# gate_a's matvec on TensorE beside the attention: runs of two slabs at half the rate in place of single slabs

## The chip, the cores and the metric

The kernel runs on one core of a Trainium2 chip. A core has five engines that run side by side, each in the order of its own instruction list: TensorE (PE, matmuls; its weight loads are shown apart as PEld), VectorE (DVE), ScalarE (ACT), GpSimd (POOL) and SyncE (SP), which here only issues DMAs. The metric is the device time of one execution in us.

## The reference

One step of one layer for 128 context tokens and 256 latent tokens, all in float32, model width 2048. Six vectors of 2048 per token group, among them gate_a, come out of a matvec of the condition with a 2048 x 12288 matrix:

```python
def _adaln(cond, ada_w, ada_b):
    mod = jax.nn.silu(cond) @ ada_w + ada_b
    return mod.reshape(cond.shape[0], N_MOD, D_MODEL)

def _layer(x, mod, ...):
    shift_a, scale_a, gate_a, shift_f, scale_f, gate_f = [mod[:, i][:, None, :] for i in range(N_MOD)]
    h = _rmsnorm(x, norm_w[0]) * (1 + scale_a) + shift_a
    q, k, v, o, g, u = jnp.split(h @ w_in, ...)
    hm, C, n, m = _mlstm_bidir(q, k, v, gates, C0, n0, m0)        # attention, 8 heads of 128, two directions
    hm = _rmsnorm(hm, mlstm_norm_w) * jax.nn.sigmoid(o)
    mix = jnp.concatenate([hm, _pool_mixer(u, ...)], axis=-1) @ w_out
    x = x + gate_a * _rmsnorm(mix, norm_w[1])
    h = _rmsnorm(x, norm_w[2]) * (1 + scale_f) + shift_f
    y = jnp.square(jax.nn.relu(h @ w1)) @ w2
    return x + gate_f * _rmsnorm(y, norm_w[3]), C, n, m
```

gate_a is needed only where the output projection is done.

## The kernel before

All 384 tokens go through each stage together. Weights come in tiles of 512 KB, 4 x 128 rows by 256 columns (`load_w`): SP loads a tile into one of three buffers (`raw_q`, `raw_k`, `raw_o`, `raw_wo`), ScalarE rounds it to a high part `hi_...`, VectorE subtracts that for a low part `lo_...` (four buffers each), and TensorE makes three matmuls of each product (lines 143 to 145). A tile's 24 matmuls of 384 columns make one step of a projection (`gemm_T`).

The program goes: the first two modulation vectors and the projections u and v; then, for four groups g of two heads, the projections q and k (`qk(g, ...)`), with the attention of the group before laid between their steps; the projection o in four groups; the output projection wo, in which x stays in 16 tiles; then the MLP. What is laid between the steps of a projection comes from generators. A `Feed` has a rate; after each step it adds the rate to what is due and calls the generator once for each whole number. `fa` holds the attention of the head groups, `ada2` the matvecs for scale_f, shift_f and half of gate_a on VectorE, `ada1` the matvec for the other half of gate_a on TensorE. `ada1` is started with the first projection and is finished in the output projection.

`ada_mat` is TensorE's way: a slab is four rows (of 16 per partition) by 256 columns of the matrix, 512 KB. Per slab there is one load on SP (line 228), and four matmuls (line 232) with a stationary operand of 32 columns, each of which stands in the trace as two records (`ada<-ada_raw,cT 128*32`). gate_a's half has 16 slabs. Behind the last of them ScalarE copies the sums, and two small matmuls (line 241) turn them. `ada_vec` is VectorE's way: a slab is 128 x 1024, one load on SP (line 269) a slab ahead, and two operations of VectorE on it (lines 280 and 282, one for each token group).

Both ways take their slabs from one ring of four buffers, tag "ada" (`N_ADA = 4`): a load waits until the slab of four loads before has been used, whichever engine used it. The order of TensorE, VectorE, ScalarE and SP in this part of the program is made by a scheduler when the kernel is built, from the order in which the code is written and from a model of when operands and buffers come free; it is fixed from then on. SP stands in front of a load until its buffer is free, and every later load on SP stands behind it.

Of the kernel before, what the change touches and what calls it, by code (L numbers as in the profile page):

```python
# [7 lines left out]
F32 = mybir.dt.float32  # L8
# [5 lines left out]
P = 128  # L14
# [13 lines left out]
N_W = 4  # L28
N_ADA = 4
# [10 lines left out]
RATE_MAT = 0.35  # L40
# [3 lines left out]
def hymba_kernel(  # L44
# [6 lines left out]
    nc = tc.nc  # L51
# [3 lines left out]
    wp = ctx.enter_context(tc.tile_pool(name="wp", bufs=3))  # L55
    slots = ctx.enter_context(tc.tile_pool(name="slots", bufs=N_SLOT))
    ada_scope = ExitStack()
    adap = ada_scope.enter_context(tc.tile_pool(name="adap", bufs=1, side="right"))
# [6 lines left out]
    def bank(name):  # L65
        return psum.tile([P, 512], F32, tag="ps", name=name)
# [145 lines left out]
    mod = const.tile([P, 6, KT, 2], F32, name="mod")  # L212
    aw = ada_w.rearrange("(p j) n -> p j n", j=16)

    def ada_mat(parts, tags=("ada",), raws=None):


        n, nk = len(parts), parts[0][2]
        w, nj = nk * P, 8 // nk
        ps = bank(f"ada_{parts[0][0]}_{parts[0][1]}")  # L220
        for b, (i, k0, _) in enumerate(parts):
            c0 = i * D + k0 * P
            for j0 in range(0, 16, nj):
                tag = tags[b % len(tags)]
                raw = raws.pop(0) if raws else None
                if raw is None:
                    raw = (wp if tag == "lo" else adap).tile([P, nj, w], F32, tag=tag, name=f"ada_raw_{i}_{k0}_{j0}", bufs=N_W if tag == "lo" else N_ADA)
                    nc.sync.dma_start(raw, aw[:, j0:j0 + nj, c0:c0 + w])
                for a in range(nj):
                    j = j0 + a  # L230
                    g = j % 4
                    nc.tensor.matmul(ps[32 * g:32 * g + 32, 0:w], cT[:, j, 6 - 2 * b:38 - 2 * b], raw[:, a, :],  # L232
                                     start=b == 0 and j < 4, stop=b == n - 1 and j >= 12)
                if b < n - 1 or j0 + nj < 16:
                    yield
        sb = adap.tile([P, 512], F32, tag="adasb", name=f"ada_sb_{parts[0][0]}_{parts[0][1]}", bufs=1)
        with tc.high_priority():
            nc.scalar.activation(sb[:, 0:w], ps[:, 0:w], AF.Copy)
        yield
        for k in range(nk):  # L240
            nc.tensor.matmul(ps[:, 256 + 8 * k:256 + 8 * k + 2 * n], sb[:, k * P:(k + 1) * P], cst[:, C_SEL, 0:2 * n], start=True, stop=True)
        for b, (i, k0, _) in enumerate(parts):
            ada_finish(i, k0, nk, ps[:, 256:256 + 8 * nk].rearrange("p (k r) -> p k r", r=8)[:, :, 2 * b:2 * b + 2])
        yield

    def ada_finish(i, k0, nk, ps):

        v = mod[:, i, k0:k0 + nk, :]
        nc.vector.tensor_tensor(
            v, ps,  # L250
            abias[:, i, k0:k0 + nk].unsqueeze(2).to_broadcast([P, nk, 2]), op=ALU.add)
        if i in (1, 4):
            w = nw[:, i // 2, k0:k0 + nk].unsqueeze(2).to_broadcast([P, nk, 2])
            nc.vector.scalar_tensor_tensor(v, v, 1.0, w, op0=ALU.add, op1=ALU.mult)
        elif i in (2, 5):
            w = nw[:, 1 if i == 2 else 3, k0:k0 + nk].unsqueeze(2).to_broadcast([P, nk, 2])
            nc.vector.tensor_tensor(v, v, w, op=ALU.mult)
# [50 lines left out]
    def first_ada():  # L308
        for k0, nk in ksteps:
            yield from ada_mat([(0, k0, nk), (1, k0, nk)], ("ada", "lo") if k0 == 0 else ("ada",))  # L310
# [66 lines left out]
    def load_chunk(s, ci, after=(), later=None):  # L377
        kind, c0, w = chunks[ci]
        ks = slice(ksteps[s][0], sum(ksteps[s]))
        if kind == "u":  # L380
            n, pieces = w, [(0, wv_in[:, ks, U0 + c0:U0 + c0 + w])]
        else:
            n, pieces = w * P, [(0, wv_in[:, ks, V0 + c0 * P:V0 + (c0 + w) * P])]
            if c0 == 6:
                pieces.append((n, wv_in[:, ks, 4 * M:4 * M + 32]))
                n += 32
        return load_w(pieces, f"{kind}_{c0}_{s}", ksteps[s][1] * n, after, later) + (n,)
# [9 lines left out]
    for s in range(NS):  # L397
        for ci, (kind, c0, w) in enumerate(chunks):
            k0, nk = ksteps[s]
            hi, lo, n = w_first if s == 0 and ci < 2 else load_chunk(s, ci, h_ins if s == 0 else ())  # L400
# [301 lines left out]
    def mid_vec():  # L702
        for i, q in ((4, 0), (4, 1), (3, 0), (3, 1), (2, 0)):
            yield from ada_vec(i, 1024 * q, 1024)

    ada1 = Feed(ada_mat([(2, 8 + 2 * b, 2) for b in range(4)]), RATE_MAT)
    ada2 = Feed(mid_vec(), RATES[0])

    def qk(g, feeds):
# [92 lines left out]
    for cols in ([0, 256], [512], [768], [1024], [1280], [1536], [1792]):  # L802
        if cols[0] in (768, 1024, 1280):
            for m in range(2):
                n = len(early)
# [71 lines left out]
    def gate_f():  # L877
        yield from ada_mat([(5, 0, 2), (5, 2, 2)], raws=early)
        for q in (1, 2, 3):
            yield from ada_vec(5, 512 * q, 512)  # L880
            if q == 1:
                vec["half"] = True
                while vec["half"]:
                    yield
        ps = bank("gfT")
        t = slot("gfT")[0:32, 0:P]
        nc.tensor.transpose(ps[0:32, 0:P], mod[:, 5].rearrange("p k g -> p (k g)"), ident)
        nc.vector.tensor_copy(t, ps[0:32, 0:P])  # L888
        nc.gpsimd.dma_start(gf_dram, t)  # L889
        yield  # L890
# [409 lines left out]
```

## Time and profile before

The median of three runs is 1694.79 us (1694.71 to 1697.43). The page below is of one execution of 1699.63 us, of which 1697.80 us are the span of the core.

| | us |
|---|---|
| profiled execution | 1699.63 |
| its span | 1697.80 |
| median of 3 runs | 1694.79 |

gate_a's 16 slabs on TensorE start at these times of that execution, in us, with the name that the instruction order gives their load (column tile and row):

| slab | us | slab | us |
|---|---|---|---|
| 8_0 | 225.65 | 8_4 | 245.88 |
| 8_8 | 263.41 | 8_12 | 281.50 |
| 10_0 | 298.42 | 10_4 | 315.10 |
| 10_8 | 334.80 | 10_12 | 346.67 |
| 12_0 | 362.81 | 12_4 | 382.06 |
| 12_8 | 397.23 | 12_12 | 416.10 |
| 14_0 | 436.24 | 14_4 | 450.25 |
| 14_8 | 459.44 | 14_12 | 472.81 |

The state updates of the attention that the prediction speaks of (`cu`) start on TensorE at 278.7, 324.9, 372.6 and 421.0 us, one for each head group.

Rows of the profile begin with the time of the start in us, the duration, the engine and the line; `out<-in` names tiles, x8 says that eight equal records follow each other, and a bracket at the end gives the time for which the engine stood idle ahead of it and who ended that. A row "A <- B: 1.9, 2, 1.1" says that A waited for B 1.9 us in all, in two waits, the longest of 1.1.

### The profile page before, as it was taken

How to read it: one execution, taken by the hardware profiler on the slowest of the kernel's cores; microseconds unless marked ns; L12 is line 12 of the kernel's file. 1: busy time of each engine (PE TensorE's matmuls, PEld its weight loads, DVE VectorE, ACT ScalarE, POOL GpSimd, SP SyncE). 2: the span in 40 equal slices, each digit the busy share in tenths (PEclk: the TensorE clock that was granted, in tenths of full speed). 3: DMA queues.
4: the chain of work that ended last, by engine and by line, in shares of the span. 5: the costliest groups of instructions: out<-in, count | busy, mean ns of one | idle time of the engine just before them, and what ended most of it. 6: DMA issues, size and time to landing. Idle time of an engine off the chain costs nothing.

```text
span 1697.8 us, 28001 instructions
## 1 busy us (share of the span) xinstructions
PE 1664.2 (98%) x11021; PEld 1581.1 (93%) x11021; DVE 1341.8 (79%) x2000; ACT 750.9 (44%) x1224; POOL 155.9 (9%) x194
## 2 busy tenths in 40 slices
PE   6999999999999999999999999999999999999997
PEld 3787899999999989988999999999999999999996
DVE  3676759898989969997798588988588588588688
ACT  4422345545433336453444444344444444444443
POOL 0000001221002223540000000000000000000120
PEclk9999999999999999999999999999999999999999
DMA  8899857777788883754455344544343443533653
GB/s 292 290 298 298 285 164 251 243 242 244 240 271 283 264 264 99 213 161 145 153 180 166 108 149 146 184 150 133 115 141 116 143 129 112 158 112 116 187 183 136
DMA packets 262291, 320.95 MB, mean 189 GB/s; under 512 B 14752, under 2 KB 231440, under 8 KB 261776
## 3 DMA queue, kind: packets, MB, share of 16 engines
q1 hardware_dynamic: 254640, 303.61, 56.8%
q0 software_dynamic: 5856, 13.69, 2.8%
q8 instruction: 86, 1.41, 0.3%
q10 hardware_dynamic: 1664, 1.87, 0.3%
q14 instruction: 45, 0.37, 0.1%
HBM read 308.61 MB, written 10.51 MB: 188 GB/s over the span
## 4 chain that ended last, share of the span: by engine, by line
PE 68%; DVE 15%; DMA 8%; issue 6%; ACT 1%; POOL 1%; SPq 0%; DVEq 0%; ACTq 0%; POOLq 0%
PE acc_w L145 9%; PE acc_w L143 9%; PE acc_w L144 9%; DVE ada_acc L282 6%; PE y L1134 4%; PE y L1135 4%; PE y L1133 4%; PE u L411 2%; DMA raw_u<-in_w_in_dram 2%; PE v L411 2%; PE y_yz L1133 2%; PE y_yz L1134 2%; PE y_yz L1135 2%; PE y L975 2%; PE y L977 2%
## 5 line engine op out<-in xcount | busy, mean ns | idle before, releaser
L144 PE MATMUL acc_w<-h2l,hi_w 128*128 128x384 f32 (+1 forms) x1024 | 345.8, 338 | 0.5 <-DVE h2l L927 0.5
L145 PE MATMUL acc_w<-h2h,lo_w 128*128 128x384 f32 (+1 forms) x1024 | 345.9, 338 | 0.0
L143 PE MATMUL acc_w<-h2h,hi_w 128*128 128x384 f32 (+1 forms) x1024 | 343.8, 337 | 1.3 <-ACT h2h L923 1.2
L135 DVE TENSOR_TENSOR lo_w<-raw_w,hi_w 128x1024 fp32r<-128x1024 f32 x152 | 185.4, 1221 | 135.7 <-ACT hi_w L134 135.6
L282 DVE SCALAR_TENSOR_TENSOR ada_acc<-ada_raw,sg,ada_acc 128x1024 f32<-128x1024 f32 (+1 forms) x240 | 259.9, 1113 | 6.7 <-DMA ada_raw<-in_ada_w_dram 6.7
L134 ACT ACTIVATE hi_w<-raw_w 128x1024 fp32r<-128x1024 f32 x152 | 160.8, 1058 | 211.8 <-PE acc_w L144 93.9
L143 PEld LDWEIGHTS acc_w<-h2h,hi_w 128*128 128x128 f32 x1024 | 192.2, 188 | 2.9 <-ACT h2h L923 2.0
L144 PEld LDWEIGHTS acc_w<-h2l,hi_w 128*128 128x128 f32 x1024 | 192.5, 188 | 1.2 <-DVE h2l L927 0.8
L145 PEld LDWEIGHTS acc_w<-h2h,lo_w 128*128 128x128 f32 x1024 | 192.4, 188 | 0.3 <-DVE lo_w L135 0.2
L1119 ACT ACTIVATE hi_t<-w 128x1024 fp32r<-128x1024 f32 x104 | 109.5, 1059 | 119.0 <-DVE w L1155 34.3
L1120 DVE TENSOR_TENSOR lo_t<-w,hi_t 128x1024 fp32r<-128x1024 f32 x104 | 126.4, 1221 | 14.4 <-ACT hi_t L1119 14.2
L1120 DVE TENSOR_TENSOR lo_b<-w,hi_b 128x1024 fp32r<-128x1024 f32 x78 | 95.2, 1221 | 39.5 <-ACT hi_b L1119 39.3
L1119 ACT ACTIVATE hi_b<-w 128x1024 fp32r<-128x1024 f32 x78 | 82.5, 1059 | 96.0 <-PE acc_w L144 62.3
L134 ACT ACTIVATE hi_wo<-raw_wo 128x1024 fp32r<-128x1024 f32 x32 | 34.0, 1063 | 84.7 <-DMA raw_wo<-in_w_out_dram 57.4
L853 ACT ACTIVATE z<-acc_w 128x384 f32<-128x384 f32 x54 | 26.3, 486 | 74.5 <-PE acc_w L145 74.5
L889 POOL DMA_DIRECT2D gf_dram<-gfT x1 | 0.5, 521 | 552.3 <-DVE gfT L888 552.3
L135 DVE TENSOR_TENSOR lo_wo<-raw_wo,hi_wo 128x1024 fp32r<-128x1024 f32 x32 | 40.4, 1268 | 9.6 <-ACT hi_wo L134 9.5
L411 PE MATMUL v<-hi_v,hh 128*128 128x384 f32 (+1 forms) x144 | 47.8, 332 | 0.0
L411 PE MATMUL v<-hi_v,hl 128*128 128x384 f32 (+1 forms) x144 | 46.5, 323 | 0.0
L411 PE MATMUL v<-lo_v,hh 128*128 128x384 f32 (+1 forms) x144 | 46.5, 323 | 0.0
L232 PE MATMUL ada<-ada_raw,cT 128*32 128x256 f32 x656 | 44.8, 392 | 1.6 <-DMA ada_raw<-in_ada_w_dram 1.5
L134 ACT ACTIVATE hi_u<-raw_u 128x1024 fp32r<-128x1024 f32 x16 | 16.8, 1058 | 63.7 <-DMA raw_u<-in_w_in_dram 62.5
(2250 smaller groups left out, 4602.9 us busy)
## 6 DMA issues: line engine op xcount, KB each, us to landing
ada_raw<-in_ada_w_dram SPq DMA_DIRECT2D x170, 512.0 KB, 4.8
raw_w<-in_w_dram SPq DMA_DIRECT2D x152, 512.0 KB, 4.3
w<-in_w_dram SPq DMA_DIRECT2D x104, 512.0 KB, 4.2
raw_wo<-in_w_out_dram SPq DMA_DIRECT2D x32, 512.0 KB, 5.0
raw_u<-in_w_in_dram SPq DMA_DIRECT2D x16, 512.0 KB, 8.6
raw_q<-in_w_in_dram SPq DMA_DIRECT2D x16, 512.0 KB, 4.8
raw_k<-in_w_in_dram SPq DMA_DIRECT2D x16, 512.0 KB, 4.8
raw_o<-in_w_in_dram SPq DMA_DIRECT2D x16, 512.0 KB, 5.2
```

Source lines behind the costliest of these rows:

```text
L134: nc.scalar.activation(hi[:, 0:n], raw[:, 0:n], AF.Copy)
L135: low = lambda: nc.vector.tensor_tensor(lo[:, 0:n], raw[:, 0:n], hi[:, 0:n].bitcast(F32), op=ALU.subtract)
L143: nc.tensor.matmul(ps, lh, rh, start=start, stop=False)
L144: nc.tensor.matmul(ps, lh, rl, start=False, stop=False)
L145: mm3.ins = nc.tensor.matmul(ps, ll, rh, start=False, stop=stop).ins
L282: nc.vector.scalar_tensor_tensor(acc[:, g, :], raw[:, a, :], cj, acc[:, g, :], op0=ALU.mult, op1=ALU.add)
L411: nc.tensor.matmul(acc[i][:, 0:n], h[k0 + k][a][:, i * P:(i + 1) * P], (hi, lo)[b][:, k, :], start=k == 0 and a + b == 0, stop=k == nk - 1 ...
L1119: nc.scalar.activation(hi, raw, AF.Copy)
L1120: nc.vector.tensor_tensor(lo, raw, hi.bitcast(F32), op=ALU.subtract)
L1133: nc.tensor.matmul(acc, xh, wh, start=start and j == 0, stop=False)
L1134: nc.tensor.matmul(acc, xh, wl, start=False, stop=False)
L1135: nc.tensor.matmul(acc, xl, wh, start=False, stop=stop and j == 3)
```

## The change

`ada_mat` gets an argument `run`. With `run=2` a call of the generator makes two loads, then the eight matmuls of both slabs, and then yields; before, a call made one load and four matmuls. The rate of `ada1` is halved, from 0.35 to 0.175 calls per step, so the two together give the same number of slabs per step. Other callers of `ada_mat` keep `run=1`. In the changed kernel the lines behind 212 have moved: line 228 is 230, 232 is 236, and from there on each line is four higher.

```diff
-    def ada_mat(parts, tags=("ada",), raws=None):
+    def ada_mat(parts, tags=("ada",), raws=None, run=1):
...
         for b, (i, k0, _) in enumerate(parts):
             c0 = i * D + k0 * P
+            ahead = []
             for j0 in range(0, 16, nj):
                 tag = tags[b % len(tags)]
-                raw = raws.pop(0) if raws else None
-                if raw is None:
-                    raw = (wp if tag == "lo" else adap).tile([P, nj, w], F32, tag=tag, name=f"ada_raw_{i}_{k0}_{j0}", bufs=N_W if tag == "lo" else N_ADA)
-                    nc.sync.dma_start(raw, aw[:, j0:j0 + nj, c0:c0 + w])
+                for j1 in range(j0, j0 + nj * run, nj) if not ahead else ():
+                    raw = raws.pop(0) if raws else None
+                    if raw is None:
+                        raw = (wp if tag == "lo" else adap).tile([P, nj, w], F32, tag=tag, name=f"ada_raw_{i}_{k0}_{j1}", bufs=N_W if tag == "lo" else N_ADA)
+                        nc.sync.dma_start(raw, aw[:, j1:j1 + nj, c0:c0 + w])
+                    ahead.append(raw)
+                raw = ahead.pop(0)
                 for a in range(nj):
...
-                if b < n - 1 or j0 + nj < 16:
+                if (b < n - 1 or j0 + nj < 16) and (j0 // nj) % run == run - 1:
                     yield
...
-    ada1 = Feed(ada_mat([(2, 8 + 2 * b, 2) for b in range(4)]), RATE_MAT)
+    ada1 = Feed(ada_mat([(2, 8 + 2 * b, 2) for b in range(4)], run=2), RATE_MAT / 2)
```

On TensorE, the third and the fourth slab (8_8 and 8_12) before: the third stands behind the decays of head group 0 (`mb`), the fourth behind its intra-chunk products (`num`), 91 rows later.

```order
L586 MATMUL mb_0_1_1_2677<-mrow_2080,pick_2081 128x384
L232 MATMUL ada_2_8_2315<-ada_raw_2_8_8_2688,cT_109 32x256 x4
L143 MATMUL acc_q_256_0_2622<-hh4_725,hi_q_256_1_2699 128x384
...
L641 MATMUL num_0_0_1_2867<-v0_85,e_0_2654 128x129 x2
L232 MATMUL ada_2_8_2315<-ada_raw_2_8_12_2881,cT_109 32x256 x4
L143 MATMUL acc_k_1280_0_2899<-hh0_266,hi_k_1280_0_2903 128x384
```

On TensorE after, at the same two places:

```order
L590 MATMUL mb_0_1_1_2677<-mrow_2080,pick_2081 128x384
L143 MATMUL acc_q_256_0_2622<-hh4_725,hi_q_256_1_2693 128x384
...
L645 MATMUL num_0_0_1_2861<-v0_85,e_0_2654 128x129 x2
L236 MATMUL ada_2_8_2498<-ada_raw_2_8_8_2875,cT_109 32x256 x4
L236 MATMUL ada_2_8_2498<-ada_raw_2_8_12_2877,cT_109 32x256 x4
L143 MATMUL acc_k_1280_0_2899<-hh0_266,hi_k_1280_0_2903 128x384
```

The third slab has gone from its place and stands directly ahead of the fourth. All pairs are like this, in the place of their second slab, but for 14_0 and 14_4, which stand together between their two places.

On SP, the loads around 360 to 372 us before. `ada_raw_4_1024_n` is VectorE's n-th slab of the second half of scale_f, `ada_raw_2_12_4` TensorE's slab 12_4, whose neighbour 12_0 has been loaded ten rows earlier.

```order
L269 DMA ada_raw_4_1024_9_3930<-in_ada_w_dram 128x1024
L128 DMA raw_k_1792_1_4022<-in_w_in_dram 128x4x256
L269 DMA ada_raw_4_1024_10_3934<-in_ada_w_dram 128x1024
L128 DMA raw_k_1792_2_4098<-in_w_in_dram 128x4x256
L228 DMA ada_raw_2_12_4_4012<-in_ada_w_dram 128x4x256
L269 DMA ada_raw_4_1024_11_4018<-in_ada_w_dram 128x1024
L269 DMA ada_raw_4_1024_12_4090<-in_ada_w_dram 128x1024
L128 DMA raw_k_1792_3_4132<-in_w_in_dram 128x4x256
```

On SP after, the same place:

```order
L273 DMA ada_raw_4_1024_9_3924<-in_ada_w_dram 128x1024
L273 DMA ada_raw_4_1024_10_3928<-in_ada_w_dram 128x1024
L128 DMA raw_k_1792_1_4022<-in_w_in_dram 128x4x256
L230 DMA ada_raw_2_12_0_4006<-in_ada_w_dram 128x4x256
L128 DMA raw_k_1792_2_4098<-in_w_in_dram 128x4x256
L230 DMA ada_raw_2_12_4_4008<-in_ada_w_dram 128x4x256
L273 DMA ada_raw_4_1024_11_4018<-in_ada_w_dram 128x1024
L128 DMA raw_k_1792_3_4132<-in_w_in_dram 128x4x256
L273 DMA ada_raw_4_1024_12_4090<-in_ada_w_dram 128x1024
```

Both slabs of the pair are loaded here, between VectorE's slabs 10 and 11, and the load of slab 12 has gone behind that of raw_k_1792_3.

On VectorE, the operations around 374 to 380 us before. `nout` and `C1` are the state updates of head group 2, `dn` its denominators:

```order
L282 SCALAR_TENSOR_TENSOR ada_acc_4_1024_3569<-ada_raw_4_1024_11_4018,sg_111,ada_acc_4_1024_3569 128x1024 x2
L282 SCALAR_TENSOR_TENSOR ada_acc_4_1024_3569<-ada_raw_4_1024_12_4090,sg_111,ada_acc_4_1024_3569 128x1024
L683 COPY nout_2082<-C1_2_0_0_3878 128x2
L683 COPY nout_2082<-C1_2_0_1_3885 128x2
L631 SCALAR_TENSOR_TENSOR C1_2_1_0_3892<-C0_2_0_3703,glast_2078,cu_2_1_0_3893 128x129 x2
L655 TENSOR_TENSOR dn_2_0_0_3909<-dn_2_0_0_3909,ecol_2076 128x2
```

On VectorE after:

```order
L286 SCALAR_TENSOR_TENSOR ada_acc_4_1024_3563<-ada_raw_4_1024_11_4018,sg_111,ada_acc_4_1024_3563 128x1024 x2
L687 COPY nout_2082<-C1_2_0_0_3872 128x2
L687 COPY nout_2082<-C1_2_0_1_3879 128x2
L635 SCALAR_TENSOR_TENSOR C1_2_1_0_3886<-C0_2_0_3703,glast_2078,cu_2_1_0_3887 128x129 x2
L286 SCALAR_TENSOR_TENSOR ada_acc_4_1024_3563<-ada_raw_4_1024_12_4090,sg_111,ada_acc_4_1024_3563 128x1024
L635 SCALAR_TENSOR_TENSOR C1_2_2_1_3892<-C0_2_1_3706,glast_2078,cu_2_2_1_3893 128x129 x2
```

The first operation on slab 12 has moved behind the two copies and the first state update. Elsewhere on VectorE single operations on slabs change places with their neighbours in the same way, up to the output projection; none is added or taken away. In the output projection the two small matmuls of line 241 stand 24 matmuls later. From there on the orders of all engines are the same in both kernels.

## The prediction

> **What bounds the kernel now.** I read the page's busy times first, then a table of four stretches, then what TensorE waited for in the stretch that the change touches, then its rows in order of time. The columns of the table are the stretch in us, its length, and busy us of PE, PEld, DVE, ACT and POOL, the granted clock, the DMA share and GB/s.
>
> ```profile
> PE 1664.2 (98%) x11021; PEld 1581.1 (93%) x11021; DVE 1341.8 (79%) x2000; ACT 750.9 (44%) x1224; POOL 155.9 (9%) x194
> 220.00:480.00 260.00, 258.96 (x1674) 245.77 (x1674) 220.89 (x366) 130.43 (x325) 41.85 (x38) 1.00 0.72 229
> 480.00:640.00 160.00, 157.41 (x957) 150.42 (x955) 137.92 (x160) 59.49 (x99) 32.82 (x31) 1.00 0.84 272
> 640.00:1697.80 1057.80, 1045.76 (x6972) 1023.26 (x6970) 845.03 (x1180) 482.59 (x672) 76.52 (x110) 1.00 0.48 146
> ```
>
> TensorE sets the end: it stands idle for 1.0 us of the 260 in which the changed work lies (220 to 480 us), and for 2.6 of the 160 behind it. VectorE is not far off, at 220.9 of 260 and 137.9 of 160. The clock is full, so it explains nothing here. The few idle moments of TensorE between 220 and 640 us are these (line waiting, for whom, us in total, times, longest):
>
> ```profile
> PE acc_wo L145 <- DVE lo_wo L135: 1.9, 2, 1.1
> PE inter L648 <- DVE hs L658: 0.7, 2, 0.5
> PE hT L697 <- DVE hs L661: 0.3, 1, 0.3
> ```
>
> They are small, but nearly all of them are waits for VectorE. At these places both engines arrive together, and time saved on TensorE alone becomes a longer wait there. That is what decides this case.
>
> **The price of a slab.** A slab is one load of gate_a's weights, four matmuls in the program, eight records of the form 128*32 in the trace. One slab alone, behind attention work and ahead of the projection, against the same seam without a slab:
>
> ```profile
> 435.70 0.61 PE L648 MATMUL inter<-C,q 128*128 128x129 f32 x4
> 436.24 0.64 PE L232 MATMUL ada<-ada_raw,cT 128*32 128x256 f32 x8
> 436.81 0.44 PE L143 MATMUL acc_o<-hh,hi_o 128*128 128x384 f32 x1
> 437.09 0.34 PE L144 MATMUL acc_o<-hl,hi_o 128*128 128x384 f32 x1
> ...
> 341.91 0.61 PE L648 MATMUL inter<-C,q 128*128 128x129 f32 x4
> 342.28 0.42 PE L143 MATMUL acc_k<-hh,hi_k 128*128 128x384 f32 x1
> 342.54 0.34 PE L144 MATMUL acc_k<-hl,hi_k 128*128 128x384 f32 x1
> ```
>
> From the first inter matmul to the second projection matmul it is 437.09 - 435.70 = 1.39 us with the slab and 342.54 - 341.91 = 0.63 without: a slab alone costs **0.76 us**. Inside a projection, between two matmuls of the same accumulation, it costs the same:
>
> ```profile
> 245.62 0.34 PE L145 MATMUL poolo<-p21h,lo_pw 128*128 128x384 f32 x1
> 245.88 0.64 PE L232 MATMUL ada<-ada_raw,cT 128*32 128x256 f32 x8
> 246.45 0.45 PE L143 MATMUL acc_k<-hh,hi_k 128*128 128x384 f32 x1
> 246.74 0.33 PE L144 MATMUL acc_k<-hl,hi_k 128*128 128x384 f32 x1
> 246.91 0.33 PE L145 MATMUL acc_k<-hh,lo_k 128*128 128x384 f32 x1
> ```
>
> Here 246.74 - 245.62 = 1.12 us, less two ordinary steps of 246.91 - 246.74 = 0.17, is 0.78. What a second slab directly behind the first costs, gate_f's run of four slabs shows:
>
> ```profile
> 627.50 1.93 PE L232 MATMUL ada<-y,cT 128*32 128x256 f32 x32
> ```
>
> Four slabs take 1.93 us, the first 0.64, so each further one takes (1.93 - 0.64) / 3 = **0.43 us**. The rest of a lone slab's 0.76 is paid at its two borders, where the tile's form changes from 128*128 to 128*32 and back.
>
> **The change, part by part.** The slabs, their last one, and the first reader of gate_a:
>
> ```profile
> L232 PE MATMUL ada<-ada_raw,cT x144: 379/379/404, 225.6 to 632.0; 128*32 128x256 f32 x144
> ...
> 472.81 0.64 PE L232 MATMUL ada<-ada_raw,cT 128*32 128x256 f32 x8
> ...
> 630.54 1.00 DVE L919 SCALAR_TENSOR_TENSOR mo<-mo,mod,tr_r 128x128 f32<-128x128 f32 x3 [1.00 <-PE tr_r L208]
> ```
>
> 144 records, less the 16 of gate_f's two slabs behind 631 us, are 16 slabs of eight. Alone they have 16 borders in and out, in pairs 8. TensorE's work falls by 8 x (0.76 - 0.43) = **2.64 us**; its bounds are 8 x 0, if the second slab pays the price of the first, and 8 x 0.76 = 6.1, if it cost nothing. I take 2.64, as the run of four is the same instruction with the same shape. The number of matmuls, DMAs and bytes is unchanged. The last slab stands at the same place; the two small matmuls that turn the result stand one projection step of 24 matmuls later, and the first reader of gate_a, line 919, starts at 630.5 us, so this is hidden by the whole output projection and costs nothing unless it came over 100 us later.
>
> How much of 2.64 reaches the end I get by following the **lead**, how much earlier the same instruction runs. Each first slab that is gone adds 0.76, each second slab that is added takes back 0.43, and wherever VectorE hands over to TensorE, the lead falls to VectorE's own. VectorE's lead in turn comes from TensorE at the state updates, where VectorE waits for ScalarE's copy of what TensorE has just made (325 us) or for the store of that copy (427 us). The rows of these hand-overs, VectorE's largest waits for POOL and for its own loads in 250 to 480 us, and its load from 500 to 540 us:
>
> ```profile
> 381.42 0.71 PE L648 MATMUL inter<-C,q 128*128 128x129 f32 x4 [0.48 <-DVE hs L658]
> 325.93 0.17 DVE L683 COPY nout<-C 128x2 f32<-128x2 f32 x1 [2.55 <-ACT C L628]
> 427.37 0.61 DVE L631 SCALAR_TENSOR_TENSOR C<-C,glast,cu 128x129 f32<-128x129 f32 x2 [1.49 <-DMA out_dram<-C]
> 524.01 0.44 PE L145 MATMUL acc_wo<-mx12h,lo_wo 128*128 128x384 f32 x1 [1.11 <-DVE lo_wo L135]
> ...
> DVE hs L661 <- POOL rsh L200: 7.0, 12, 0.8
> ...
> DVE ada_acc L282 <- DMA ada_raw<-in_ada_w_dram: 3.3, 3, 1.8
> ...
> 500.00:540.00 40.00, 38.09 (x216) 37.30 (x215) 40.00 (x33) 12.09 (x18) 5.85 (x4) 1.00 0.89 293
> ```
>
> - The slabs' times are in the table of the profile section. At 325 us three pairs are done, 3 x 0.33 = 0.99, but the wait at 308 (0.3 us, above) has already cut the lead by 0.33: TensorE and VectorE both have 0.66.
> - At 381 TensorE has 0.66 + 0.76 - 0.43 + 0.76 = 1.75. VectorE's waits from 330 to there are those of 0.6 to 0.8 for POOL, none for TensorE, so it still has 0.66, and the wait of 0.48 grows to 1.6. Lead 0.66.
> - The pair at 382 takes it to 0.23, the slab gone at 397 to 0.99, the pair at 416 to 0.56. VectorE takes this 0.56 over at 427.
> - By 475 TensorE has 0.56 + 2 x 0.33 = 1.2. VectorE works without a gap in the last row, and at 524 TensorE waits for it: the lead that goes on is **0.56 us**, the wait there grows from 1.1 to about 1.8.
>
> Behind 640 us the order of all engines is the same and TensorE sets the pace, so 0.56 reaches the end. Of the 2.64 saved, 2.1 turn into longer waits. If these waits were no barrier, all 2.64 would get through, and with the 0.48 of the wait at 381 gone too, 3.1.
>
> **The ring of four buffers.** Slabs for TensorE share four buffers with the slabs that VectorE multiplies (line 269). Before, one of the four waits for TensorE; after, two do, from their load to the pair's turn, and VectorE's loads have the other two. Take the second half of the head group at 360 to 382 us. SP's issues, VectorE's uses of what lands, and the times to landing (min, median, max) in this stretch:
>
> ```profile
> 359.89 0.33 SPq L269 DMA_DIRECT2D ada_raw<-in_ada_w_dram  x1
> 364.38 0.38 SPq L228 DMA_DIRECT2D ada_raw<-in_ada_w_dram  x1
> 364.81 4.10 SPq L269 DMA_DIRECT2D ada_raw<-in_ada_w_dram  x2
> ...
> 367.27 1.27 DVE L282 SCALAR_TENSOR_TENSOR ada_acc<-ada_raw,sg,ada_acc 128x1024 f32<-128x1024 f32 x1
> 369.60 2.47 DVE L282 SCALAR_TENSOR_TENSOR ada_acc<-ada_raw,sg,ada_acc 128x1024 f32<-128x1024 f32 x2
> 373.73 3.66 DVE L282 SCALAR_TENSOR_TENSOR ada_acc<-ada_raw,sg,ada_acc 128x1024 f32<-128x1024 f32 x3
> ...
> DMA to landing us min/median/max: 3.2/4.6/7.3
> ```
>
> Before, slab 11 is loaded at 364.8, when TensorE lets its buffer go, and slab 12 at 368.6. After, both wait one release of VectorE longer: slab 11 for the end of the use at 367.27 (368.5), slab 12 for the end of 369.60 + 2.47 (372.1). With 4.6 us they land at 373.1 and 376.7. They are used at 373.73 and, as the third operation from there, at about 376.2; in the new order VectorE does two state copies and an update ahead of it, some 0.7 us. So they are just in time. Of the other seven pairs, worked out alike, two have a load that is late by about half a us. I price the ring at **0** with 0 to 1 us against it; weights behind these loads in SP's queue (raw_k, raw_o) wait for the same releases as before. The cover that hides it is VectorE's other work between two slabs.
>
> The sum: 1699.63 (the profiled execution; its span is 1697.80) - 0.56 = 1699.1. That execution is 4.8 above the median of the three runs, 1694.79; carried to it, **1694.2 us**.
>
> **Rivals.**
> - *All of it gets through.* VectorE's order changes too, and if its hand-overs come earlier, TensorE's 2.64 to 3.1 us reach the end: 1691.7 to 1692.2. For it: VectorE is idle for 39 of the 260 us. Against it: the waits above are all on VectorE, and those at 524 and behind lie in a stretch where it has no gap.
> - *The ring starves VectorE* (the slower side). With two buffers a slab costs VectorE 4.6 for the load, 0.4 for the issue and 2.5 for its two operations, 7.5 us for a buffer's round and so 3.75 per slab, and in the rows above it takes two between 369.6 and about 376.2, one in 3.3. From where two loads in a row miss their use, each pair costs a wait like the one for the load at 467 us, 1.84 us in the row below, handed on at 381, 429 or 524. In four of eight pairs that is 7.4 - 2.6 = 4.8 us: about 1699.6.
>
> ```profile
> 467.58 1.29 DVE L282 SCALAR_TENSOR_TENSOR ada_acc<-ada_raw,sg,ada_acc 128x1024 f32<-128x1024 f32 x1 [1.84 <-DMA ada_raw<-in_ada_w_dram]
> SPq L269 <- DVE ada_acc L282: 106.3, 47, 4.0
> SPq L228 <- DVE ada_acc L282: 23.0, 9, 3.5
> ```
>
> The last two rows show SP standing at these loads until VectorE lets a buffer go, with everything behind them standing too. The Trainium skill, "DMA: Bandwidth & Descriptors", section "Anatomy of one DMA — SWDGE (gpsimd) path", states this as a rule: a DMA engine waits for no semaphore, the wait is made on the issuing sequencer ahead of the dispatch. By that rule two waiting loads in a row hold up the projection's weights as well, and the rival's 1699.6 is what would follow; the trace agrees on where the wait is made, and its single slabs cannot show whether the weights come late.
> - *It does nothing on TensorE.* If the second slab costs 0.76 as well, the sum is 0: 1694.8. Against it stands the run of four.
>
> **How the numbers follow.** Forecast, a small gain of 0 to 1.5 us: 0.55. All gets through (1.5 to 3.1 us): 0.20. Nothing on TensorE: 0.05. Ring or another wait on VectorE costs more than it saves: 0.20, of this 0.13 beyond 0.2%. A difference under 0.2% (3.4 us) can't be told from none here; the three runs of before themselves span 2.7 us. Only a second slab near the bound of no cost gets above 3.4 us: faster 0.10, taken out of the second case; same 0.77; slower 0.13. The range goes from 1691.6, all with the wait at 381, up to 1697.4, the highest run of before and half of the starved ring.
>
> **What would show it.** TensorE's groups of line 236 have 16 records and take about 1.07 us, eight of them; a group of 0.64 twice speaks for the last rival. The waits of lines 648 and 145 behind VectorE (0.7 and 1.9 us) grow to about 2.6 in all at 381 and 524 if the lead is cut as I say, and stay or shrink if all gets through. VectorE's wait for its slabs, 3.3 us in three times, stays below 5; at 10 or more the ring starves. I am wrong if line 128's loads come late or if anything behind 640 us changes.

## The result, and the profile after

The changed kernel takes **1700.16 us** (median of 15 runs, 1698.05 to 1706.83), the kernel before 1696.62 us in the same comparison (15 runs, 1694.71 to 1699.10). The ratio is 1.0025, with a 95% interval of 1.0018 to 1.0033: slower by a quarter of a per cent, where I had forecast 1694.2 and a small gain. Two repeats gave 1.0032 (1.0020 to 1.0044) and 1.0018 (1.0008 to 1.0028).

The page's busy times and the three stretches of the changed kernel, in the columns of the prediction's table:

```profile
PE 1662.1 (98%) x11021; PEld 1582.1 (93%) x11021; DVE 1341.0 (79%) x2000; ACT 752.0 (44%) x1224; POOL 156.4 (9%) x194
220.00:480.00 260.00, 256.04 (x1673) 246.20 (x1672) 221.27 (x368) 130.49 (x326) 42.02 (x38) 1.00 0.71 228
480.00:640.00 160.00, 158.20 (x960) 151.15 (x960) 137.35 (x159) 59.14 (x97) 33.35 (x31) 1.00 0.83 274
640.00:1699.30 1059.30, 1047.32 (x6975) 1024.52 (x6973) 845.56 (x1180) 483.93 (x673) 76.31 (x110) 1.00 0.48 146
```

TensorE's busy time on the page has fallen by 2.1 us; a second profile of the kernel before has 1662.6 us, so this sum alone shows little. Its idle time between 220 and 480 us has grown from 1.0 to 4.0 us. The waits in that stretch and the one behind it, and behind them the row of one pair:

```profile
PE inter L652 <- DVE hs L662: 3.1, 2, 1.9
PE hT L701 <- DVE hs L665: 0.9, 1, 0.9
PE acc_wo L145 <- DVE lo_wo L135: 0.8, 1, 0.8
...
DVE C L635 <- DMA out_dram<-C: 3.6, 2, 2.4
...
DVE ada_acc L286 <- DMA ada_raw<-in_ada_w_dram: 2.5, 4, 1.1
```

```profile
246.18 1.07 PE L236 MATMUL ada<-ada_raw,cT 128*32 128x256 f32 x16
```

The pair costs 1.07 us, so the second slab costs the 0.43 that I took. VectorE's wait for its slabs has not grown (2.5 us, before 3.3). What has grown is TensorE's wait for `hs`, from 0.7 to 3.1 us, in two waits. `hs` is VectorE's first read of the sums `num` that TensorE has just made for a head group; until it is done, TensorE has no `bank` (the kernel's name for a buffer of such sums) for the next `inter`, the products with the states. The two waits are at the hand-overs of head groups 2 and 3:

```profile
381.66 0.71 PE L652 MATMUL inter<-C,q 128*128 128x129 f32 x4 [1.20 <-DVE hs L662]
...
431.56 0.71 PE L652 MATMUL inter<-C,q 128*128 128x129 f32 x4 [1.86 <-DVE hs L662]
```

Before, the first of them was 0.48 us, in the prediction's row at 381.42, and the second this:

```profile
429.61 0.71 PE L648 MATMUL inter<-C,q 128*128 128x129 f32 x4 [0.26 <-DVE hs L658]
```

VectorE ahead of that second hand-over, in the order of time, before:

```profile
424.59 1.28 DVE L282 SCALAR_TENSOR_TENSOR ada_acc<-ada_raw,sg,ada_acc 128x1024 f32<-128x1024 f32 x1
427.37 0.61 DVE L631 SCALAR_TENSOR_TENSOR C<-C,glast,cu 128x129 f32<-128x129 f32 x2 [1.49 <-DMA out_dram<-C]
427.89 0.22 DVE L656 RECIPROCAL dn<-dn 128x2 f32<-128x2 f32 x2
428.02 1.27 DVE L282 SCALAR_TENSOR_TENSOR ada_acc<-ada_raw,sg,ada_acc 128x1024 f32<-128x1024 f32 x1
429.21 0.60 DVE L658 SCALAR_TENSOR_TENSOR hs<-num,dn,hs 128x128 f32<-128x128 f32 x2
429.73 1.22 DVE L135 TENSOR_TENSOR lo_o<-raw_o,hi_o 128x1024 fp32r<-128x1024 f32 x1
```

and after:

```profile
424.37 1.28 DVE L286 SCALAR_TENSOR_TENSOR ada_acc<-ada_raw,sg,ada_acc 128x1024 f32<-128x1024 f32 x1
428.05 0.61 DVE L635 SCALAR_TENSOR_TENSOR C<-C,glast,cu 128x129 f32<-128x129 f32 x2 [2.39 <-DMA out_dram<-C]
428.57 0.23 DVE L659 TENSOR_TENSOR dn<-dn,ecol 128x2 f32<-128x2 f32 x2
428.71 1.28 DVE L286 SCALAR_TENSOR_TENSOR ada_acc<-ada_raw,sg,ada_acc 128x1024 f32<-128x1024 f32 x1
429.90 0.22 DVE L660 RECIPROCAL dn<-dn 128x2 f32<-128x2 f32 x2
430.04 1.21 DVE L135 TENSOR_TENSOR lo_o<-raw_o,hi_o 128x1024 fp32r<-128x1024 f32 x1
431.16 0.60 DVE L662 SCALAR_TENSOR_TENSOR hs<-num,dn,hs 128x128 f32<-128x128 f32 x2
```

Two things are to be seen. VectorE's second state update (`C`) waits until the store of the first new state has left its buffer (the tiles `C` have five buffers, and a head group uses six), and `hs` stands behind that wait. And between the update and `hs` stood one long operation before (a slab, 1.27 us) and stand two now (a slab and `lo_o`). From the start of the update's second operation (x2 in a row says that it holds two) to the end of the first `hs` it is 1.9 us before and 3.2 now. `lo_o` stood behind `hs`. In group 2 it is also 3.2 us in place of 1.9: there a slab operation that stood ahead of the update has come between. Before:

```profile
379.24 0.59 DVE L631 SCALAR_TENSOR_TENSOR C<-C,glast,cu 128x129 f32<-128x129 f32 x2
...
379.89 1.21 DVE L135 TENSOR_TENSOR lo_k<-raw_k,hi_k 128x1024 fp32r<-128x1024 f32 x1
381.03 0.34 DVE L658 SCALAR_TENSOR_TENSOR hs<-num,dn,hs 128x128 f32<-128x128 f32 x1
```

and after:

```profile
378.14 0.60 DVE L635 SCALAR_TENSOR_TENSOR C<-C,glast,cu 128x129 f32<-128x129 f32 x2
...
378.80 1.28 DVE L286 SCALAR_TENSOR_TENSOR ada_acc<-ada_raw,sg,ada_acc 128x1024 f32<-128x1024 f32 x1
...
380.13 1.21 DVE L135 TENSOR_TENSOR lo_k<-raw_k,hi_k 128x1024 fp32r<-128x1024 f32 x1
381.25 0.61 DVE L662 SCALAR_TENSOR_TENSOR hs<-num,dn,hs 128x128 f32<-128x128 f32 x2
```

In these two profiles neither update had to wait for the store, so in group 2 it is the order that makes `hs` late. Counted from the start of TensorE's state matmuls `cu`, the first `hs` of group 2 ends after 8.8 us before and 9.5 now, that of group 3 after 8.6 and 10.2.

### The profile page after: what moved, and what is told of

Its sections match the earlier page's. It is cut to its first block, busy times and chain, and to the rows that moved or that the text cites. A ratio compares the mean times of both kernels' runs of the same rounds, so it can differ in the third digit from the quotient of the medians.

```text
span 1699.3 us, 27993 instructions
## 1 busy us (share of the span) xinstructions
PE 1662.1 (98%) x11021; PEld 1582.1 (93%) x11021; DVE 1341.0 (79%) x2000; ACT 752.0 (44%) x1224; POOL 156.4 (9%) x194
## 4 chain that ended last, share of the span: by engine, by line
PE 77%; DVE 10%; DMA 6%; issue 4%; ACT 1%; POOL 1%; SPq 0%; DVEq 0%; ACTq 0%; POOLq 0%
PE acc_w L143 9%; PE acc_w L145 9%; PE acc_w L144 9%; PE y L1138 4%; PE y L1139 4%; PE y L1137 4%; DVE ada_acc L286 3%; PE v L415 2%; PE u L415 2%; DMA raw_u<-in_w_in_dram 2%; PE y_yz L1137 2%; PE y_yz L1138 2%; PE y_yz L1139 2%; PE y L979 2%; PE y L981 2%
```

## The experiments

All ratios are to the kernel before in runs of the same call, with the 95% interval. To see where in the run time goes, I compare the starts of the same projection matmul in two traces; the table gives the distance to the run `b_again`, set to 0 at 217 us (ahead of the first slab; the programs are alike up to there). Each row is one execution: `noload2`, `fix2` and `C6fix2` were profiled in the fastest of their runs, `a_again` and `C6before` in the slowest, and ahead of 217 us the traces lie up to 2.7 us on either side of `b_again`. A row tells where time goes in its stretch, the ratio what the change is worth.

| kernel | at 369 us | 384 | 414 | 460 | 535 | ratio |
|---|---|---|---|---|---|---|
| before (first profile) | +0.5 | +0.7 | +0.7 | +1.2 | +2.2 | |
| after (first profile) | -1.0 | +0.3 | -0.5 | +1.0 | +1.7 | 1.0025 |
| a_again | -1.2 | +3.6 | +2.8 | +4.5 | +5.0 | 1.0032 (1.0020 to 1.0044) |
| a_third | -1.8 | -0.5 | -1.3 | +1.9 | +2.5 | 1.0018 (1.0008 to 1.0028) |
| loads2 | +0.5 | -0.1 | -0.1 | +0.5 | +0.5 | 1.0012 (1.0003 to 1.0020) |
| hold1 | +2.9 | +2.7 | +2.7 | +3.5 | +3.9 | 1.0022 (1.0013 to 1.0031) |
| noload1 | +0.5 | +0.5 | +0.5 | +0.5 | +0.5 | 1.0002 (0.9993 to 1.0011) |
| noload2 | -2.0 | -0.5 | -1.2 | +1.8 | +2.1 | 1.0007 (0.9998 to 1.0016) |
| nofix2 | -2.0 | -2.1 | -2.1 | -1.8 | -0.7 | 1.0001 (0.9992 to 1.0010) |
| fix2 | -1.5 | -1.3 | -1.4 | -1.1 | +1.1 | 1.0011 (1.0002 to 1.0020) |
| fix1 | +0.6 | 0.0 | 0.0 | 0.0 | +1.0 | 1.0005 (0.9996 to 1.0014) |
| order1 | +0.6 | +0.8 | +0.8 | +1.1 | +1.1 | 1.0004 (0.9995 to 1.0013) |
| order2 | +1.0 | +2.1 | +2.1 | +3.0 | +3.0 | 1.0003 (0.9992 to 1.0013) |
| C6before | 0.0 | -0.6 | -0.7 | -0.6 | -0.6 | 0.9989 (0.9980 to 0.9998) |
| C6before_b | 0.0 | -0.6 | -0.6 | -0.6 | -0.6 | 0.9991 (0.9982 to 1.0001) |
| C6after | -1.6 | -1.5 | -2.2 | -2.9 | -2.7 | 0.9982 (0.9974 to 0.9991) |
| C6after_b | -1.6 | -1.0 | -1.7 | -2.4 | -1.2 | 0.9989 (0.9980 to 0.9998) |
| C6fix2 | -1.5 | -1.7 | -2.4 | -3.1 | -2.9 | 0.9988 (0.9979 to 0.9997) |

All three rows of the changed kernel are ahead at 369 us and lose it at the two hand-overs, from 369 to 384 and from 414 to 460.

**Is the difference there at all?** The changed kernel and the kernel before, unaltered:

> The changed kernel once more, unaltered. Theory R (ring: pairs hold two of the four buffers, VectorE's loads lose their slack, so that in most executions some load is late and VectorE hands over late): again 2 to 5 us above before, 1698.5 to 1701, spread wider than before's, and in a second profile VectorE's wait for ada_raw and TensorE's waits for hs differ from those of the first. Theory N (the difference is a matter of the executions that happened to be compared): within 1 us of before. Theory S (the changed order of VectorE makes the hand-overs at 381 and 429 us later by itself, whenever the loads land): 2 to 5 us above before with a narrow spread, and TensorE's waits for hs the same 3.1 us in two as in the first profile.

> The kernel before once more, unaltered, against itself. All theories: ratio 1.000 within 0.001. If it comes out 0.2% off, theory N holds: a difference of that size says nothing.

`a_again` 1700.44, `b_again` 1696.82 us, 1.0010 (1.0001 to 1.0019) of itself. So the difference is real, and a tenth of a per cent is what this comparison makes out of nothing. In `a_again` TensorE waits 4.3 us for `hs`, 2.14 of it at group 2, where a slab for VectorE landed 0.82 us late on top of the rest:

```profile
377.38 1.29 DVE L286 SCALAR_TENSOR_TENSOR ada_acc<-ada_raw,sg,ada_acc 128x1024 f32<-128x1024 f32 x1 [0.82 <-DMA ada_raw<-in_ada_w_dram]
...
382.09 1.08 PE L652 MATMUL inter<-C,q 128*128 128x129 f32 x4 [2.14 <-DVE hs L662]
```

**The ring.** Loads in pairs, matmuls one slab at a time, and runs of four:

```diff
-                if (b < n - 1 or j0 + nj < 16) and (j0 // nj) % run == run - 1:   # loads2
+                if b < n - 1 or j0 + nj < 16:
-    ada1 = Feed(ada_mat([(2, 8 + 2 * b, 2) for b in range(4)], run=2), RATE_MAT / 2)
+    ada1 = Feed(ada_mat([(2, 8 + 2 * b, 2) for b in range(4)], run=2), RATE_MAT)      # loads2
+    ada1 = Feed(ada_mat([(2, 8 + 2 * b, 2) for b in range(4)], run=4), RATE_MAT / 4)  # run4
```

> Loads in pairs as in the change, but TensorE's slabs one at a time at the full rate of 0.35, so TensorE's own work is that of before (1664.2 us busy) and nothing is saved at the borders. Theory R: the pairing of the loads alone costs, so 1698 to 1703, at or above the changed kernel, with little slack on VectorE's loads. Theory S and theory N: the place of TensorE's slabs is that of before, so within 1 us of before, 1696 to 1697.5.

> Runs of four slabs at a quarter of the rate: TensorE saves 12 borders of 0.33 us = 4.0 us of work, and a run takes all four buffers. Theory R: VectorE has no buffer from a run's first load to its turn, so more than the changed kernel, 1702 to 1712, VectorE's waits for ada_raw and SP's for its slabs grow several times over. Theory S and N: no worse than the changed kernel, 1695 to 1700.

`loads2` 1697.63 us, 1.0012 where `b_again` has 1.0010 in the same call: loading in pairs costs nothing that can be seen. `run4` 1711.3 us, 1.0096 (1.0081 to 1.0110): with all four buffers in one run the ring does decide. What VectorE waits for its slabs is only 4.2 us there; what comes late are the projection's weights, which stand behind the slab loads in SP's queue. ScalarE's waits for weights from 220 to 640 us in `run4`:

```profile
ACT hi_k L134 <- DMA raw_k<-in_w_in_dram: 12.3, 4, 4.6
ACT hi_o L134 <- DMA raw_o<-in_w_in_dram: 10.2, 6, 3.0
ACT hi_q L134 <- DMA raw_q<-in_w_in_dram: 3.9, 1, 3.9
```

26.4 us in all, against 4.0 before and 3.5 in the changed kernel (9.1 and 5.0 in its other two profiles, 8.5 in `fix1` with single slabs). TensorE waits 3.2 us for `lo_k` in `run4`, and in none of those others for `lo_q`, `lo_k` or `lo_o`. So this is what the ring's rival looks like, and the pairs do not show it, but for the one late slab of `a_again`. The rule of the Trainium skill that the prediction weighed ("DMA: Bandwidth & Descriptors", section "Anatomy of one DMA — SWDGE (gpsimd) path": the wait is made by the issuing sequencer) agrees with `run4`, where what stands behind the waiting loads comes late; the section is on DMAs that GpSimd issues, here SP issues them.

Next the hold alone, and the pairs without the ring: `hold1` puts off the last matmul of each first slab to the second slab's turn; `noload1` and `noload2` are before and after with TensorE's slabs read from a constant, which leaves that half of gate_a out.

```diff
+                todo = [(j0 + a, raw[:, a, :]) for a in range(nj)]                # hold1, in before
+                if hold and (j0 // nj) % 2 == 0:
+                    todo, kept = todo[:-1], todo[-1:]
+                elif hold:
+                    todo = kept + todo
...
+            still, raws = cst[:, 0:2, :].rearrange('p a b -> p (a b)'), None      # noload1, noload2
```

> Single slabs as before, but the last matmul of the first slab of each pair is put off to the second slab's turn, so that the first slab's buffer is held as long as in the changed kernel, while the orders of the engines are those of before but for a handful of rows. Theory R: 1698 to 1702, as the changed kernel or above it (nothing is saved at the borders). Theory S: within 1.5 us of before, TensorE's waits for hs under 1 us.

> The kernel before, but TensorE's 16 slabs of gate_a are not loaded: their matmuls read a constant tile instead (that half of gate_a is left out). The ring of four belongs to VectorE alone; the orders of TensorE, VectorE, ScalarE and GpSimd are those of before. Control for the next run. Every theory: at or a little below before, 1692 to 1697, as 8 MB of loads are gone.

> The changed kernel with the same loads left out: pairs on TensorE, orders of TensorE, VectorE, ScalarE and GpSimd exactly those of the changed kernel, ring free. Theory R (ring): without the ring's hold the pairs' saving comes through, so 0.5 to 2.6 us below the control. Theory S (the order of VectorE, which the pairs have shifted, reads TensorE's sums late at the hand-overs): 3 to 5 us above the control, and TensorE's waits for hs at 381 and 429 us still add up to over 3 us.

`hold1` 1699.88 us, but not for the ring: its second turns take ten records in place of eight, and 1.05 us in place of 0.64, while the first turns with six take no less.

```profile
264.43 0.63 PE L236 MATMUL ada<-ada_raw,cT 128*32 128x256 f32 x6
282.52 1.05 PE L236 MATMUL ada<-ada_raw,cT 128*32 128x256 f32 x10
```

That is 8 x 0.41 = 3.3 us of TensorE's own work, and the median stands 3.3 us above before; the hold is left with about nothing. The run changes TensorE's own work, so it says this only after that subtraction. `noload2`: at 369 us the pairs are 2.0 us ahead of `b_again`, and 4 x 0.33 + 0.76 = 2.08 were due there; then the two hand-overs take it back without any ring, with waits for `hs` of 1.50 and 1.86 us. It ends at 1697.77 us against 1696.97 of `noload1`, between what the two theories expected; the intervals of the two ratios overlap, so the 0.80 is not told from none. Of the 2.64 saved plus the 3.5 us lost by the change, some 6 us, about 2.64 + 0.80 = 3.4 need no ring, with an uncertainty of some 2 us.

**VectorE's order.** `fix2` is the changed kernel with two slabs of VectorE kept behind `hs` of groups 2 and 3, `fix1` the same in the kernel before, `nofix2` is `fix2` with `noload2`'s constant.

```diff
+    behind = {(4, 1024, 12): (2, 0, 0), (3, 0, 5): (3, 0, 0)}
...
+                            if (i, c, t) in behind:
+                                es.enter_context(tc.issue_after(read[behind[i, c, t]]))
                             nc.vector.scalar_tensor_tensor(acc[:, g, :], raw[:, a, :], cj, acc[:, g, :], op0=ALU.mult, op1=ALU.add)
```

> The changed kernel with its pairs and loads, TensorE's order untouched, but VectorE's operations on two slabs (slab 12 of the second half of scale_f, slab 5 of the first half of shift_f) are put behind the read of TensorE's sums (hs) of head groups 2 and 3. Theory S: TensorE's waits for hs at 381 and 429 us fall from 3.1 to 4.3 to under 1.5 us, and the time falls by 2 to 5 us, to 1694 to 1698. Theory R: the loads are as before in the changed kernel, so 1699 to 1701.

> The kernel before with VectorE's slabs 12 and 5 behind hs, as fix2 does it for the changed kernel. Theory S: before waits only 0.4 to 0.5 us for hs at 381, so 0 to 1 us below before; fix2's gain on the changed kernel was the larger, as the shifted order was there. If it falls by 2 us or more as well, fix2 has mended something that the change did not break.

> Pairs on TensorE, their loads left out as in noload2 (that half of gate_a is left out), and VectorE's operations on slabs 12 and 5 put behind hs as in fix2. With ring and order both out of the way, the saving of 2.6 us at the borders should come through if those two are the whole loss: 1.5 to 3 us below noload1's ratio of 1.000, that is 0.998 to 0.999. If a third thing eats the saving, it stays at 1.000 to 1.001.

`fix2` 1697.97 us, 2.2 below the first median of the changed kernel; TensorE's waits for `hs` fall to 0.3 us, which shows the cause of these waits. Its ratio of 1.0011 is that of `b_again`, but the interval overlaps that of `a_third` (from 1.0008), so how much time comes back is known only roughly. In its profile 2.2 us are lost again from 460 to 535, with a wait of 1.4 for `lo_wo` where I had let the lead end. `fix1` 1697.05, no gain, so it mends only what the change broke. `nofix2` 1696.41, 1.0001 (0.9992 to 1.0010): at 384 us it is 2.6 us ahead of `noload1`, behind 460 it loses half of its lead, and the median shows no gain that could be told. With ring and order both out of the way I had expected 0.998 to 0.999, so these two are not the whole loss.

Then the other direction, the order alone. `order1` moves two slab operations in the kernel before across 351 us; `order2` moves one slab operation in each of groups 2 and 3 from ahead of the second state update to behind it.

```diff
+    behind = {(4, 1024, 5): (1, 2)}                                               # order1
+    behind = {(4, 1024, 12, 1): 2, (3, 0, 5, 1): 3}                               # order2
...
+                                es.enter_context(tc.issue_after(last_C[behind[i, c, t, g]]))
+                                es.enter_context(tc.high_priority())
```

> The kernel before (single slabs, its loads, TensorE's order unchanged), but VectorE's two operations on slab 5 of the second half of scale_f are put behind the norm (hs by rsh) of head group 1, where the changed kernel has them, so that VectorE has 16 instead of 14 slab operations between 351 us and the first hs of group 2. Theory S: TensorE's wait for hs at 381 us grows from 0.4 or 0.5 us to 1.5 to 2.5, and the time by 1 to 3 us, to 1697.5 to 1700. Theory R: nothing of the ring's hold has changed, so within 1 us of before.

> The kernel before (single slabs and its loads), but in head groups 2 and 3 one operation of VectorE on a slab that stands ahead of the second state update, where VectorE waits for the store, is put behind it, so that two long operations stand between the update and hs, as in the changed kernel. Theory S in its second form (work taken out of the cover of the store's wait and put between it and hs): from the second update to the end of the first hs 3.2 us in place of 1.9, TensorE's waits for hs at 381 and 429 us 1.2 to 2.2 us each, time 2 to 4 us above before, 1698 to 1700.5. Theory R: within 1 us of before.

> The changed kernel a third time, beside order2 on one chip. All theories: 1.002 to 1.003 of before. Second form of S: 3.2 us from the second update to hs in groups 2 and 3, waits for hs of 3 to 4.5 us in two.

`order1` 1696.24 us, nothing: my first form of the theory was wrong, two more slab operations ahead of `hs` made no difference here. `order2` at group 3, and TensorE's wait for `hs` in it:

```profile
427.43 0.61 DVE L636 SCALAR_TENSOR_TENSOR C<-C,glast,cu 128x129 f32<-128x129 f32 x2 [1.14 <-DMA out_dram<-C]
427.95 1.28 DVE L287 SCALAR_TENSOR_TENSOR ada_acc<-ada_raw,sg,ada_acc 128x1024 f32<-128x1024 f32 x1
429.15 0.22 DVE L661 RECIPROCAL dn<-dn 128x2 f32<-128x2 f32 x2
429.28 1.21 DVE L135 TENSOR_TENSOR lo_o<-raw_o,hi_o 128x1024 fp32r<-128x1024 f32 x1
430.40 0.61 DVE L663 SCALAR_TENSOR_TENSOR hs<-num,dn,hs 128x128 f32<-128x128 f32 x2
```

```profile
PE inter L653 <- DVE hs L663: 2.1, 2, 1.5
```

The mechanism is there: two long operations, 3.1 us, waits of 2.1 in place of 0.7, 1.1 and 1.0 us lost at the two hand-overs in the table. The median, 1697.97, is 1.6 above before where I had expected 2 to 4, and the ratio takes in no change. I take it that with single slabs TensorE arrives later and the same lateness of VectorE costs less, so that the order and the earlier arrival together make the waits of 1.2 to 2.1; this is argued, not shown. `a_third`, beside it: 1699.73 us, waits for `hs` of 3.2 us, `hs` 3.2 us behind the update in both groups.

**The store.** Six buffers for the states in place of five (in this line and in that of the old states), in the changed kernel, in the kernel before, and in `fix2`:

```diff
-            out = att.tile([P, 2, 129], F32, tag="C", name=f"C1_{hp}_{i}_{d}", bufs=5)
+            out = att.tile([P, 2, 129], F32, tag="C", name=f"C1_{hp}_{i}_{d}", bufs=6)
```

> The changed kernel with six buffers in place of five for the attention's states C, so that the sixth state of a head group no longer waits for the store of the first. If VectorE's wait for that store, with hs queued behind it, is what makes the hand-over at 429 us late (theory S's second half), the wait of TensorE there falls under 0.8 us and the time to 1695 to 1699. If it is the ring, VectorE's time is spent at the slabs in place of the store, and it stays at 1699 to 1701.

> The kernel before with six buffers for C, the control of the run above: TensorE waits little for VectorE there (0.3 to 0.7 us for hs), so 0 to 1 us below before. More than 2 us below would say that the store's wait costs every version and is no part of the change's loss.

> The changed kernel with six buffers for C and with the two slabs of VectorE behind hs, both together. Theory S: TensorE's waits for hs under 0.8 us in all, a time of 1692 to 1696, below before by up to the 2.6 us saved. Theory R: still 2 us or more above before.

> Pairs with six buffers for C, once more. If the pairs' saving of 2.6 us comes through where VectorE is never late, 1.5 to 3 us below the next run; TensorE waits under 0.8 us for hs.

> Single slabs with six buffers for C, once more: 1 to 2 us below before, as the first time.

`C6after` 1693.97 us, repeated 1694.11; `C6before` 1695.02 and 1695.12; `C6fix2` 1693.82, 0.9988 (0.9979 to 0.9997). All medians are below before, by little more than the tenth of a per cent that comes out of nothing; but the changed kernel with one more buffer is some 6 us faster than without, which is clear of it. VectorE in `C6after` at group 3, and TensorE's waits from 220 to 640 us:

```profile
418.54 1.11 DVE L635 SCALAR_TENSOR_TENSOR C<-C,glast,cu 128x129 f32<-128x129 f32 x4
419.57 0.22 DVE L659 TENSOR_TENSOR dn<-dn,ecol 128x2 f32<-128x2 f32 x2
...
420.32 1.26 DVE L286 SCALAR_TENSOR_TENSOR ada_acc<-ada_raw,sg,ada_acc 128x1024 f32<-128x1024 f32 x1
421.50 0.60 DVE L662 SCALAR_TENSOR_TENSOR hs<-num,dn,hs 128x128 f32<-128x128 f32 x2
```

```profile
PE acc_wo L145 <- DVE lo_wo L135: 0.5, 1, 0.5
PE acc_w L143 <- ACT h2h L927: 0.5, 1, 0.5
PE hT L701 <- DVE hs L665: 0.3, 1, 0.3
PE adaf L303 <- ACT adav_sb L299: 0.3, 1, 0.3
```

All four state updates go without a wait, and no wait for `hs` at an `inter` is left. Counted from `cu`, the first `hs` of group 3 ends after 5.35 us. From 217 to 535 us this execution is 2.66 us ahead of `b_again` and 2.05 ahead of `C6before`, which has the same buffers; in the profiles of the repeats it is 1.2 and 0.6, with a wait of 0.5 left for `hs`. With pairs against without, the two calls give 1.05 and 1.01 us; their ratios overlap (0.9982 and 0.9989, then 0.9989 and 0.9991), so the pairs' worth in a kernel without that wait is a gain of about 1 us that these runs do not separate from none. The sixth buffer also moves rows of VectorE, so wait and order were not taken apart here.

## Why the prediction was wrong

- **The price of the second slab** was right: 1.07 us for a pair, eight times, and at 369 us `noload2` has the 2.0 us that were due. (The rows at 245 us, read as the middle of an accumulation, lie between the pool's projection `poolo` and `acc_k`; the size does not hang on it.)
- **Behind 475 us** the last slab, the two small matmuls and gate_a's first reader cost nothing, as forecast. "Anything behind 640 us" does change a little, though the orders are the same: from the matmul at 920 us in `b_again` to the last one of lines 143 to 145, at 1620, the three profiles of the changed kernel take 0.6 to 0.8 us more than `b_again`, mostly in steps of hundredths, where eight of the nine other profiles with single slabs agree with it to 0.05. `fix1`, also with single slabs, takes 0.6 more, so it is not the pairs as such; the cause was not tried.
- **The wait at 308 us** grew from 0.3 to 0.9, more than the 0.33 that I had taken from the lead, and the wait at 381 from 0.48 to 1.20; I had said 1.6. The wait of 1.1 at 524, which was to grow to 1.8, is gone, and the 0.8 some 10 us behind it is as before: there was no lead left to cut.
- **The step that failed** is the lead's second half: "The pair at 382 takes it to 0.23, ... VectorE takes this 0.56 over at 427". The hand-over at 429 us was left out. Its wait of 0.26 us stood in the row of 0.7 in two, of which I used the 0.48 alone. And I took it that a hand-over can only cap a gain at VectorE's own lead; it turned the lead into a loss, 1.86 us of waiting, since VectorE itself came later. In two of the three profiles of the changed kernel such a wait also brings half the clock for 3.41 us, an estimated 1.7 us more (last section), for which the sum had no term.
- **Why VectorE came later** stood in part in the rows that I quoted. I asked of them whether slab 12 would land in time, and gave the new order itself no term in the sum; the cover that I named, "VectorE's other work between two slabs", was for the ring. The question was what stands between the state update, which can wait for the store, and `hs`, which TensorE waits for. One long operation (1.2 to 1.3 us) had come between the two: in group 2 a slab's, from ahead of the update, in group 3 `lo_o`, from behind `hs`. In group 3 the store also landed later, 6.6 us behind the start of `cu` in place of 6.3 (5.7 in `b_again`). With two slabs held behind `hs`, some 2 us come back (`fix2`); with the wait for the store gone, 6 us (`C6after`). The order alone, in `order2`, lengthens the waits but costs a time that the runs do not tell from none.
- **The ring at 0** held on the whole. VectorE's waits for its slabs are 2.5, 3.1 and 1.5 us in the three profiles of the changed kernel. In `a_again` 0.82 us of them went into the hand-over at 381, within the 0 to 1 us that I had set against the 0. The rival that the ring starves VectorE came near the time (1699.6) by luck: its waits in four of eight pairs did not take place.
- **"The clock is full, so it explains nothing"** held for the first profiles before and after, but not for the two repeats of the changed kernel, as the last section shows.
- **The base.** The profile of before was a long execution not only by chance of its start: from 217 to 535 us it took 2.2 us longer than `b_again`, in those very waits. Against it the changed kernel's first profile is 0.5 us ahead at 535, just the lead of 0.56 that I forecast, but by luck: the waits at 381 and 429 took the lead away, and the wait at 524 of that long execution gave it back. Counting the lead against it and carrying it to the median made the loss look smaller than it is.

What is left open: the changed kernel loses some 2.6 to 4 us more than `noload2`, each against its control. The late slab in `a_again` and the waits of 0.9 and 0.7 at 308 us in two of the three profiles, which `noload2` lacks, are part of it; whether the rest is the buffers or the traffic of 8 MB was not taken apart.

## What to carry to other kernels

Where a change moves instructions, look on the engine that hands over for a wait with a needed result queued behind it: work that comes to stand between that wait and the result can make the receiving engine wait, though nothing was added. A lead that reaches a hand-over can become a loss there, so count every wait in that row, the small ones too, for they name the places where both engines already arrive together. And a buffer that takes the wait away was worth more here, some 6 us, than a better order around it, some 2.

## What the runs showed of the hardware

A wait of TensorE can cost more than its length. In `a_again`, the stretch around the wait of 2.14 us at 381 us, in the columns of the first table of stretches, and the pair in it:

```profile
378.87:382.28 3.41, 1.16 (x7) 0.97 (x8) 3.41 (x11) 1.65 (x4) 0.12 (x1) 1.00 0.44 129
382.28:385.70 3.42, 3.42 (x22) 1.92 (x22) 2.91 (x6) 1.82 (x9) 1.44 (x2) 0.50 0.90 290
385.70:389.10 3.40, 3.40 (x21) 3.40 (x21) 3.40 (x9) 0.90 (x4) 0.00 (x0) 1.00 0.95 295
```

```profile
383.10 1.94 PE L236 MATMUL ada<-ada_raw,cT 128*32 128x256 f32 x16
```

Behind a stretch of 3.41 us in which TensorE was busy for 1.16, the granted clock is 0.50 for 3.41 us, and the pair takes 1.94 us in place of 1.07. Half of 3.41 us, an estimated 1.7 us, comes on top of the wait. The same stands behind the waits of 1.98 us in `a_third` (430.47 to 433.88) and 1.86 in `noload2` (428.15 to 431.56), and twice in `run4`; in the first profile after, a wait of 1.86 had no such consequence. None of the ten profiles with single slabs has it between 220 and 640 us. The Trainium skill, "TensorE: Matmul & The Clock Gate", section "Part 1: The HAM clock gate (the "warmup" mystery)", speaks of free-running windows of about 3.4 us and of the slow clock after an idle one; the length agrees, but here a window in which TensorE was partly busy was enough.

The store of the first new state lands 6.6 to 7.3 us after the start of the state matmuls of group 3 in the nine traces with pairs, and 5.3 to 6.4 in the ten with single slabs. The cause was not tried.
